# Two-layer hybrid decoder trunk: the last four chunks of the first layer's down product become two block pairs

## The chip, the cores and the metric

The program runs on one core of one Trainium2 chip. The metric is the device time of one execution in microseconds (us). A core has a matrix engine (PE, with its weight loads shown apart as PEld), VectorE (DVE), ScalarE (ACT), GpSimd (POOL) and SyncE (SP), which here issues nearly all DMAs. Each engine works through its own list of instructions in order and waits on semaphores for the others. PE multiplies a 128x128 weight tile by a moving tile of up to 512 columns and writes into PSUM, which has eight banks of 128x512 numbers here.

## The reference

Batch 1, 512 tokens, width 1024, two layers. Each layer ends in the MLP, of which the change touches the second product; the next layer begins with a norm and a projection of the same `x`:

```python
def hybrid_layer(x, g_mix, w_in, sinks, w_a, w_b, w_out, g_mlp, w_up, w_down):
    h = rmsnorm(x, g_mix)
    z = h @ w_in
    ...
    x = x + mixed @ w_out
    h2 = rmsnorm(x, g_mlp)
    x = x + jnp.square(jax.nn.relu(h2 @ w_up)) @ w_down     # w_up 1024x4096, w_down 4096x1024
    return x
```

## The kernel before

**Layout.** Activations lie transposed: `x` is 8 chunks of 128 rows (channels) by 512 columns (tokens), in SBUF. Every factor of a product is a pair of tiles, `hi` (the value rounded to the type that PE takes) and `lo` (the rest), and one product is three matmuls: hi by hi, hi by lo, lo by hi (`products`, L332 to L334). So one output chunk over 1024 channels is 24 matmuls of 512 columns.

**Weights.** They come in units of 128x1024. `unit_order` lists the units in the order in which they are used; `load_until` issues their DMAs into `raw` tiles (three buffers), and `split_until` makes `hi` on ACT (L286) and `lo` on DVE (L287), three units ahead of use.

**The MLP.** The 4096 hidden channels are done in four quarters. `mlp_sequence` alternates a pair of w_up chunks of quarter q+1 with two w_down chunks of quarter q. The hidden values of a quarter are called u in the code (`up[q]`): a raw tile `z` of two chunks, squared on ACT and split into `hi` and `lo`. Only the last quarter's w_down product stands alone. In layer 0 it is `group` for output chunks 0 to 3 (four units, four PSUM banks open at once, 96 matmuls) and then `chunk` for 4, 5, 6 and 7. The tail of each chunk is `put_down(c, True)`: add the bank to `x` (DVE, L1436), `scaled_input` (a split of gain times x into the next layer's input, one ACT and one DVE instruction), `squared_input` (a square on ACT, an add on DVE) and a DMA of `x[c]` to HBM (`spill`). Layer 1 has its own ending, `end`.

**Block pairs.** For w_b, w_out and most of w_up the kernel has another form, `narrow_pair` (and `wide_pair`): two output chunks at once as a 2x2 block product with seven block products in place of eight. Tokens and channels are halved, so a block product is four channel tiles by 256 tokens; with three matmuls each, a narrow pair is 84 matmuls of 256 columns where two chunks are 48 of 512. It takes the weights in four parts, of which three halves are sums that DVE makes (`add_part`, L252 to L260, four 128x512 instructions a pair), and it takes three combined forms of the moving side, made by `sum_input` from the raw tiles (four 128x512 adds on DVE, then two splits of 128x1024 on ACT and DVE), which is called twice for 1024 channels. It uses three PSUM banks, `a`, `b` and `e`: `a` is filled first, copied into `b` by ACT, and the rest is added up in these banks and in two SBUF tiles.

**PSUM and order.** `ps_mm` has five banks, `ps_aux` three. The order on each engine is not the order of the code: the program is built with a scheduler that places every instruction by a timeline of its own, so what stands where must be read from the built program. Waits are found from the buffers.

Of the kernel before, what the change touches and what calls it, by code (L numbers as in the profile page):

```python
# [18 lines left out]
P = 128  # L19
T = 512  # L20
D = 1024
KD = D // P
DEPTH = 2
# [7 lines left out]
D_FF = 4096  # L31
# [19 lines left out]
ASIDE = 48  # L51
FIRST_WIDE, LAST_WIDE = 6, 32
BETWEEN = (0, 2, 4, 5)
PARKED = (("w_b", 0), ("w_b", 2), ("w_out", 6), ("w_up", 4), ("w_up", 6))
H = T // 2
CROSSED = (0, 1, 4, 5, 2, 3, 6, 7)


def unit_order():

    def plain(name, *at):
        return [(name, i) for i in range(*at)]

    def pairs(src, *firsts):
        return [("pair", j, part, src) for j in firsts for part in range(4)]

    order = plain("w_in", 26) + plain("w_a", 4) + plain("w_in", 26, 46)
    order += pairs("w_b", 0, 2) + plain("w_b", 4, 8)
    order += plain("w_out", 2) + pairs("w_out", 2, 4, 6)
    for what, q, i in mlp_sequence():  # L70
        if what == "first":
            order += plain("w_up", 4)
        elif what == "pair":
            order += pairs("w_up", 8 * q + 2 * i)
        elif what == "down":
            order += plain("w_down", 8 * q + 2 * i, 8 * q + 2 * i + 2)
        else:
            order += plain("w_down", 8 * q, 8 * q + 8)
    return order


# [46 lines left out]
def decoder(ctx, tc, xT, x_first, w_in, w_a, w_b, w_out, w_up, w_down, tables, decay, band, triangles, g_last, out):  # L128
# [34 lines left out]
    spill, aside = (dram.tile([P, KD, T], F32, name=n) for n in ("spill", "aside"))  # L163


    order = [(layer, *u) for layer in range(DEPTH) for u in unit_order()]
    raws, parts, homes = {}, {}, []
    state = {"next": 0, "loaded": 0, "split": 0}

# [433 lines left out]
    def layer_body(layer):  # L603
# [722 lines left out]
        form = form_of(by_form)  # L1326

        up = [[] for _ in range(4)]
        up_slots = [[] for _ in range(4)]

        def put_up(ps):
# [80 lines left out]
        def pair(q, i, late):  # L1412

            c = 8 * q + 2 * i
            pool = ps_aux if i % 2 == 0 else ps_mm
            turn = iter(range(7))

            def step(ins):
                now = next(turn)
                while late and now == BETWEEN[4 - len(late)]:  # L1420
                    with tc.issue_after(ins), tc.issue_after(last_low[0]):
                        late.pop(0)()

# [28 lines left out]
        for what, q, i in mlp_sequence():  # L1452
            if what == "first":
                late = group("w_up", layer, xs, [put_up] * 4, first_hooks())
            elif what == "pair":
                pair(q, i, late)
                if (q, i) == (3, 3):
                    old_input()
                    for t, _ in homes_x:
                        slots.give(*t[1])  # L1460
            elif what == "down":
                if (layer, q, i) == (DEPTH - 1, 2, 2):
                    turning = turns(0)
# [12 lines left out]
    new_input()  # L1476
# [73 lines left out]
def _swapped(u):  # L1550
    return np.concatenate([u[:, UNIT // 2 :], u[:, : UNIT // 2]], 1)
# [34 lines left out]

def _half_grouped(w):
    r = np.arange
    return _units_group(w, r(T)) + _units_chunks(w, T + r(T))


def _stack(w, of):
# [75 lines left out]
```

## Time and profile before

| what | value |
|---|---|
| median of three runs | 1468.94 us (1468.91 to 1469.76) |
| profiled execution, first to last instruction | 1467.5 us |
| granted clock of PE over the span | 1.000 |
| DVE, ACT busy over the span | 79%, 56% |
| last quarter of w_down, layer 0, first matmul of `group` | 688.55 us |
| last chunk's add to `x` | 733.70 us |
| first matmul of the sum for layer 1's norm (ssq) | 744.60 us |

The page gives the profiled execution by its span of 1467.5 us; the runs' median lies 1.4 us above it. In rows of the trace the first number is the start in us from the span's start, the second the duration, then engine, line, operation, tiles by name, shape; in brackets the idle time of the engine ahead of the instruction and what ended it. A matmul's end is modelled, so the distance from one matmul's start to the next is its cost. In rows of windows each engine has busy us and instruction count, then the granted clock, the DMA share and GB/s.

### The profile page before, as it was taken

What the parts mean: (1) busy time and instruction counts of PE and PEld (TensorE: products, weight loads), DVE (VectorE), ACT (ScalarE), POOL (GpSimd) and SP (SyncE); (2) the same over time, 40 slices, a digit from 0 to 9 for tenths busy, and PEclk for the clock granted to TensorE, in tenths of its full rate; (3) what the DMA queues carried; (4) which work ended last, traced back from release to release, by engine and by line L of the source; (5) the groups of instructions that cost most, each with busy time, mean ns of one, the idle gap of its engine ahead of it and who ended that gap; (6) DMA issues with size and microseconds to landing.
All of it is one profiled execution on the core that took longest, in us unless ns stands there. A gap on an engine that the chain in (4) does not pass through costs nothing.

```text
span 1467.5 us, 20166 instructions
## 1 busy us (share of the span) xinstructions
PE 1461.0 (100%) x7434; PEld 1246.4 (85%) x7434; DVE 1161.6 (79%) x1912; ACT 814.6 (56%) x1306; POOL 3.7 (0%) x14
## 2 busy tenths in 40 slices
PE   9999999999999999999999999999999999999998
PEld 7888888888988888888888888888989888888887
DVE  7998778678988787776678977786899877877774
ACT  7657356654684445444456653666547754455544
POOL 0000000000000000000000000000000000000000
PEclk9999999999999999999999999999999999999999
DMA  6423843356443332333543258323654432333373
GB/s 227 134 87 101 280 166 98 104 171 210 130 120 125 101 115 88 107 108 115 165 121 102 86 168 285 107 95 107 191 197 123 144 101 87 125 105 101 108 200 108
DMA packets 73346, 198.65 MB, mean 135 GB/s; under 512 B 8712, under 2 KB 8864, under 8 KB 73248
## 3 DMA queue, kind: packets, MB, share of 16 engines
q1 hardware_dynamic: 72960, 196.84, 42.5%
q8 instruction: 58, 0.95, 0.3%
q10 hardware_dynamic: 288, 0.52, 0.1%
q14 instruction: 40, 0.33, 0.1%
HBM read 173.73 MB, written 20.98 MB: 133 GB/s over the span
## 4 chain that ended last, share of the span: by engine, by line
PE 99%; DVE 0%; issue 0%; POOLq 0%; ACT 0%; DVEq 0%; ACTq 0%
PE mm L334 24%; PE mm L332 23%; PE mm L333 23%; PE mm L1356 11%; PE mm L1357 6%; PE rv L332 2%; PE rv L334 2%; PE rv L333 2%; PE score L864 1%; PE r L332 1%; PE r L334 1%; PE r L333 1%; PE pT L819 0%; PE pv L846 0%; PE pv L845 0%; PE warm L311 0%
## 5 line engine op out<-in xcount | busy, mean ns | idle before, releaser
L333 PE MATMUL mm<-r,hi 128*128 128x512 f32 (+1 forms) x1568 | 572.5, 367 | 0.0
L332 PE MATMUL mm<-r,hi 128*128 128x512 f32 (+1 forms) x1568 | 569.9, 367 | 0.0
L334 PE MATMUL mm<-r,lo 128*128 128x512 f32 (+1 forms) x1568 | 563.9, 367 | 0.2
L286 ACT ACTIVATE hi<-raw 128x1024 fp32r<-128x1024 f32 (+1 forms) x334 | 333.9, 1002 | 377.8 <-PE mm L333 206.9
L287 DVE TENSOR_TENSOR lo<-raw,hi 128x512 fp32r<-128x512 f32 (+1 forms) x335 | 384.3, 1150 | 110.8 <-ACT hi L286 109.4
L334 PEld LDWEIGHTS mm<-r,lo 128*128 128x128 f32 x1568 | 293.6, 188 | 48.8 <-DVE lo L287 1.4
L332 PEld LDWEIGHTS mm<-r,hi 128*128 128x128 f32 x1568 | 294.1, 188 | 46.5 <-ACT r L342 0.2
L333 PEld LDWEIGHTS mm<-r,hi 128*128 128x128 f32 x1568 | 294.3, 188 | 46.0
L1356 PE MATMUL mm<-r,hi 128*128 128x512 f32 x728 | 252.0, 391 | 0.0
L1357 PE MATMUL mm<-r,lo 128*128 128x256 f32 x728 | 200.3, 277 | 0.0
L1356 PEld LDWEIGHTS mm<-r,hi 128*128 128x128 f32 x728 | 136.5, 188 | 28.7 <-ACT mm L1383 0.2
L1357 PEld LDWEIGHTS mm<-r,lo 128*128 128x128 f32 x728 | 136.7, 188 | 3.2 <-DVE lo L287 0.6
L1429 ACT ACTIVATE z<-z 128x512 f32<-128x512 f32 x56 | 32.5, 624 | 51.8 <-DVE z L1409 51.8
L1436 DVE TENSOR_TENSOR x<-x,mm 128x512 f32<-128x512 f32 x56 | 37.7, 686 | 28.1 <-PE mm L334 28.1
L334 PE MATMUL rv<-hi,r 128*128 128x512 f32 x128 | 49.8, 389 | 0.0
L333 PE MATMUL rv<-lo,r 128*128 128x512 f32 x128 | 49.8, 389 | 0.0
L332 PE MATMUL rv<-hi,r 128*128 128x512 f32 x128 | 49.8, 390 | 0.0
L339 ACT ACTIVATE r<-z 128x512 fp32r<-128x512 f32 x64 | 38.5, 619 | 16.3 <-DVE z L1090 16.1
L340 DVE TENSOR_TENSOR r<-z,r 128x512 fp32r<-128x512 f32 x64 | 42.9, 685 | 4.7 <-ACT r L339 4.3
L891 ACT ACTIVATE sm<-sm,st 128x256 f32<-128x256 f32 (+1 forms) x64 | 30.1, 472 | 19.0 <-DVE st L879 18.8
L1409 DVE SCALAR_TENSOR_TENSOR z<-z,rstd 128x512 f32<-128x512 f32 x52 | 35.6, 685 | 0.6
L340 DVE TENSOR_TENSOR r<-sums,r 128x1024 fp32r<-128x1024 f32 x24 | 28.9, 1216 | 0.0
(270 smaller groups left out, 1679.2 us busy)
## 6 DMA issues: line engine op xcount, KB each, us to landing
raw<-w_in_in SPq DMA_DIRECT2D x89, 512.0 KB, 3.6
raw<-w_down_in SPq DMA_DIRECT2D x64, 512.0 KB, 3.6
raw<-w_up_in SPq DMA_DIRECT2D x32, 512.0 KB, 3.9
raw<-w_up_in SPq DMA_DIRECT2D x60, 256.0 KB, 2.9
raw<-w_a_in SPq DMA_DIRECT2D x8, 512.0 KB, 6.5
ahead<-w_b_in SPq DMA_DIRECT2D x8, 512.0 KB, 5.4
park_w_b<-ahead SPq DMA_DIRECT2D x16, 256.0 KB, 5.9
ahead<-w_up_in SPq DMA_DIRECT2D x8, 512.0 KB, 5.7
```

Of the source, the lines that this page charges most:

```text
L286: nc.scalar.activation(hi[:, at], raw[:, at], AF.Copy)
L287: last_low[:] = [nc.vector.tensor_tensor(lo[:, at], raw[:, at], f32(hi[:, at]), ALU.subtract).ins]
L332: nc.tensor.matmul(ps, ah, bh, start=start and i == 0, stop=False, **more)
L333: nc.tensor.matmul(ps, ah, bl, start=False, stop=False, **more)
L334: nc.tensor.matmul(ps, al, bh, start=False, stop=stop and i == n - 1, **more)
L339: nc.scalar.activation(hi, src, AF.Copy)
L340: nc.vector.tensor_tensor(lo, src, f32(hi), ALU.subtract)
L1356: nc.tensor.matmul(both, hi[:, c], m, start=start and k == 0, stop=False, **more)
L1357: nc.tensor.matmul(ps[:, :H], lo[:, c], m[:, 0, :], start=False, stop=k == 3 and start, **more)
L1409: nc.vector.scalar_tensor_tensor(z[:, :, at], z[:, :, at], 0.0, factor, ALU.max, ALU.mult)
L1429: nc.scalar.activation(z[:, i, :], z[:, i, :], AF.Square)
L1436: nc.vector.tensor_tensor(x[:, c, :], x[:, c, :], ps, ALU.add)
```

## The change

In layer 0, last quarter, chunks 4 to 7 of the w_down product become two narrow pairs (4, 5) and (6, 7). The weights of these four units are stored with every second unit's halves swapped, and listed as pairs. The raw tiles of u of this quarter are kept: the first three go to HBM (into `aside`) as they are made and come back (`again`), the fourth stays in SBUF; from them `sum_input` makes the three combined forms into four groups of slots. The tail of a chunk (`finish_x`) is delayed and let in at two places within the next pair. Layer 1 is as it was.

```diff
+FIRST_LATE = 4
...
-            order += plain("w_down", 8 * q, 8 * q + 8)
+            order += plain("w_down", 8 * q, 8 * q + FIRST_LATE) + pairs("w_down", *range(8 * q + FIRST_LATE, 8 * q + 8, 2))
...
             up_slots[q].extend(own)
+            if q == 3 and layer < DEPTH - 1:
+                if c < D_FF // P - 2:
+                    nc.sync.dma_start(aside[:, c - 24 : c - 22, :], z)
+                else:
+                    last_up.append(z)
...
             else:
+                delayed.clear()
+                homes_u = [forms_home() for _ in range(4)]
+                by_form_u = [h[1] for h in homes_u]
+
+                def again(k):
+                    two = big("again")
+                    nc.sync.dma_start(two, aside[:, k : k + 2, :])
+                    return two
+
+                sum_input(by_form_u, [again(0), again(4)], 0)
+                sum_input(by_form_u, [again(2), last_up[0]], 2)
                 new_input()
                 all_of(group("w_down", layer, up[q], [put_down(c, True) for c in range(4)]))
-                for c in range(4, KD):
-                    chunk("w_down", layer, up[q], put_down(c, True))
+
+                def block_u(half, tokens):
+                    at = slice(tokens * H, tokens * H + H)
+                    return [tuple(m[:, at] for m in up[q][k]) for k in range(4 * half, 4 * half + 4)]
+
+                def finish_x(c):
+                    scaled_input(c, g_mix + 2)
+                    squared_input(c, g_mix + 2)
+                    nc.sync.dma_start(spill[:, c, :], x[:, c, :])
+
+                for c in range(FIRST_LATE, KD, 2):
+                    narrow_pair(ps_aux if c % 4 else ps_mm, delayed_step(), form_of(by_form_u), block_u, add_to_x(c))
+                    delayed.extend(partial(finish_x, c + i) for i in range(2))
+                all_of(delayed)
+                delayed.clear()
+                for t, _ in homes_u:
+                    slots.give(*t[1])
                 slots.give(*up_slots[q])
```

Three places in the built programs matter. Lines of the changed kernel are numbered 3 or 4 higher than before (L287 becomes L290, L1436 becomes L1445).

The first is DVE's list behind the last scaling of u with 256 tokens (L1409, L1413). `lo`, `raw` and `z` are weight rest, weight tile and u's raw tile; `sums` are u's combined forms. Before:

```order
862 L1409 SCALAR_TENSOR_TENSOR z<-z,rstd 128x2x256
863 L287 TENSOR_TENSOR lo<-raw,hi 128x1024
864 L1363 TENSOR_TENSOR z<-mm,side 128x256
865 L287 TENSOR_TENSOR lo<-raw,hi 128x1024
866 L1409 SCALAR_TENSOR_TENSOR z<-z,rstd 128x2x256
867 L287 TENSOR_TENSOR lo<-raw,hi 128x1024
868 L340 TENSOR_TENSOR r_80<-z,r_80 128x512 x2
869 L287 TENSOR_TENSOR lo<-raw,hi 128x1024
870 L1436 TENSOR_TENSOR x<-x,mm 128x512 x3
```

Now, from the same instruction on:

```order
862 L1413 SCALAR_TENSOR_TENSOR z<-z,rstd 128x2x256
863 L629 TENSOR_TENSOR sums<-again 128x512
864 L632 TENSOR_TENSOR sums<-again 128x512
865 L630 TENSOR_TENSOR sums<-again,sums 128x512
866 L633 TENSOR_TENSOR sums<-again,sums 128x512
867 L343 TENSOR_TENSOR r_84<-sums,r_84 128x4x256
868 L629 TENSOR_TENSOR sums<-again 128x512
869 L343 TENSOR_TENSOR r_89<-sums,r_89 128x4x256
870 L290 TENSOR_TENSOR lo<-raw,hi 128x1024
871 L1367 TENSOR_TENSOR z<-mm,side 128x256
872 L290 TENSOR_TENSOR lo<-raw,hi 128x1024
873 L1413 SCALAR_TENSOR_TENSOR z<-z,rstd 128x2x256
```

Seven instructions of the forms stand ahead of the weight split that was next before, and the third tile from HBM (row 868) is read ahead of it.

The second is further down the same list: from the first weight sum of the pair (4, 5) to the adds of the group's banks to `x`. Of these rows only a split, the two of u (r_80) and the adds stood there before.

```order
876 L632 TENSOR_TENSOR sums<-z,again 128x512
877 L258 TENSOR_TENSOR raw_6415<-raw 128x512
878 L343 TENSOR_TENSOR r_80<-z,r_80 128x512
879 L633 TENSOR_TENSOR sums<-z,sums 128x512
880 L343 TENSOR_TENSOR r_80<-z,r_80 128x512
881 L262 TENSOR_TENSOR raw_6539<-raw 128x512
882 L263 TENSOR_TENSOR raw_6539<-raw_6415 128x512
883 L290 TENSOR_TENSOR lo<-raw,hi 128x1024
884 L343 TENSOR_TENSOR r_82<-sums,r_82 128x4x256
885 L290 TENSOR_TENSOR lo<-raw_6415,hi 128x1024
886 L343 TENSOR_TENSOR r_86<-sums,r_86 128x4x256
887 L1445 TENSOR_TENSOR x<-x,mm 128x512 x3
```

Ahead of these rows stand 874 (L255, the first weight sum) and 875 (L630, a form), both of 128x512. The adds of the group's banks now stand behind 13 instructions that begin with row 874; before, they stood behind one split and the two of u.

The third is PE at the end of the group, where the first pair begins. Before, chunk 4 began in the fifth bank among the last matmuls of the group (r_80 is u's last tile, r_87 its first):

```order
3530 L332 MATMUL mm<-r_87,hi 128x512 [waits DVE_49,Activation_49]
3531 L333 MATMUL mm<-r_87,hi 128x512
3532 L332 MATMUL mm<-r_80,hi 128x512 [waits Activation_49]
3533 L332 MATMUL mm<-r_80,hi 128x512 x3
3534 L334 MATMUL mm<-r_87,lo 128x512 [waits DVE_49]
```

Now the pair's bank `a` begins there with two matmuls and goes on with the ten below, and bank `e` is begun right behind it (r_84 is a form of u):

```order
3551 L337 MATMUL mm<-r_87,lo 128x256 [waits DVE_49]
3552 L335 MATMUL mm<-r_87,hi 128x256
3553 L336 MATMUL mm<-r_87,hi 128x256
3554 L337 MATMUL mm<-r_87,lo 128x256
3555 L335 MATMUL mm<-r_83,hi 128x256
3556 L336 MATMUL mm<-r_83,hi 128x256
3557 L337 MATMUL mm<-r_83,lo 128x256
3558 L335 MATMUL mm<-r_83,hi 128x256
3559 L336 MATMUL mm<-r_83,hi 128x256
3560 L337 MATMUL mm<-r_83,lo 128x256
3561 L335 MATMUL mm<-r_84,hi 128x256 [waits DVE_49]
```

The wait of row 3561 is for a bank: `a`, `b` and `e` of this pair come from `ps_mm`, whose five banks hold the group's four, so `b` and `e` are banks of the group, and `e` is free when DVE has added the group's second bank to `x` (the second of row 887 above).

More of the change, by code (lines that the diff above doesn't have):

```diff
@@ L56, with unit_order @@
 CROSSED = (0, 1, 4, 5, 2, 3, 6, 7)
-def unit_order():
+def unit_order(last):
     def plain(name, *at):
@@ L76, in unit_order @@
             order += plain("w_down", 8 * q + 2 * i, 8 * q + 2 * i + 2)
+        elif last:
+            order += plain("w_down", 8 * q, 8 * q + 8)
         else:
-            order += plain("w_down", 8 * q, 8 * q + 8)
+            order += plain("w_down", 8 * q, 8 * q + FIRST_LATE) + pairs("w_down", *range(8 * q + FIRST_LATE, 8 * q + 8, 2))
     return order
@@ L163, in decoder @@
     spill, aside = (dram.tile([P, KD, T], F32, name=n) for n in ("spill", "aside"))
-    order = [(layer, *u) for layer in range(DEPTH) for u in unit_order()]
+    order = [(layer, *u) for layer in range(DEPTH) for u in unit_order(layer == DEPTH - 1)]
     raws, parts, homes = {}, {}, []
@@ L1328, in layer_body @@
         up = [[] for _ in range(4)]
+        last_up = []
         up_slots = [[] for _ in range(4)]
@@ L1588, in _half_grouped @@
     r = np.arange
-    return _units_group(w, r(T)) + _units_chunks(w, T + r(T))
+    paired = _units_chunks(w, r(FIRST_LATE * P, D))
+    return _units_group(w, r(T)) + [_swapped(u) if i % 2 else u for i, u in enumerate(paired)]
 def _stack(w, of):
```

## The prediction

> **What bounds the kernel now.** I read the page's shares and chain first, then windows over the stretch that changes, then the single rows there.
>
> ```profile
> PE 1461.0 (100%) x7434; PEld 1246.4 (85%) x7434; DVE 1161.6 (79%) x1912; ACT 814.6 (56%) x1306; POOL 3.7 (0%) x14
> PE 99%; DVE 0%; issue 0%; POOLq 0%; ACT 0%; DVEq 0%; ACTq 0%
> 690.94:738.50 47.56, 47.56 (x214) 39.42 (x213) 28.99 (x39) 21.49 (x31) 0.00 (x0) 1.00 0.49 159
> 370.00:412.00 42.00, 41.91 (x304) 39.36 (x303) 38.32 (x56) 30.60 (x48) 0.00 (x0) 1.00 0.38 111
> ```
>
> PE is the chain: 99% of it, and the third row has PE busy for all 47.56 us of the last quarter, at clock 1.00. So a matmul saved there is time saved, and a wait of PE there is time lost. DVE works 28.99 of the 47.56 us (61%). The fourth row is the w_out product, three narrow pairs with the same tails as the new ones: DVE at 38.32 of 42.00 us (91%), and PE still has next to no gap. That is the best case for the change, and the mark to compare DVE's new load with.
>
> **What PE saves.** Out go 4 x 24 = 96 matmuls of 512 columns, in come 2 x 84 = 168 of 256.
>
> ```profile
> 728.26 0.69 DVE L1436 TENSOR_TENSOR x<-x,mm 128x512 f32<-128x512 f32 x1 [2.03 <-PE mm L334]
> 733.70 0.69 DVE L1436 TENSOR_TENSOR x<-x,mm 128x512 f32<-128x512 f32 x1 [2.04 <-PE mm L334]
> 372.44 0.28 PE L332 MATMUL mm<-r,hi 128*128 128x256 f32 x1
> 379.51 0.28 PE L332 MATMUL mm<-r,hi 128*128 128x256 f32 x1
> L333 PEld LDWEIGHTS mm<-r,hi 128*128 128x128 f32 x1568 | 294.3, 188 | 46.0
> ```
>
> Two chunks end 733.70 - 728.26 = 5.44 us apart: 24 matmuls, 0.2267 each. In w_out 60 narrow matmuls lie between 372.44 and 379.51: 0.1178 each. So 168 x 0.1178 - 96 x 0.2267 = 19.79 - 21.76 = **-1.97 us**, the whole gain, 0.13% of the time. Weight loads take 188 ns a piece but overlap, as the spacing of 0.1178 shows. The Trainium skill ("TensorE: Matmul & The Clock Gate", section "The mechanism", the list of what overlaps) says that weight loads overlap running matmuls only when row groups differ; with its figure of 107 ns for 128 columns ("LDWEIGHTS (loading the stationary operand)") beside the matmuls, an estimate would be 168 x 0.107 - 96 x 0.107 = 7.7 us more, so 5.7 us slower in all. By that rule 0.1178 could not be; the trace disagrees, and the sum goes by the row.
>
> **What DVE gets.** These rows give its pace: the distance between starts, back to back.
>
> ```profile
> 716.20 1.22 DVE L287 TENSOR_TENSOR lo<-raw,hi 128x1024 fp32r<-128x1024 f32 x1
> 717.34 0.74 DVE L343 SCALAR_TENSOR_TENSOR r<-x,r 128x512 fp32r<-128x512 f32 x1
> 718.00 0.68 DVE L429 TENSOR_TENSOR acc<-acc,sq 128x512 f32<-128x512 f32 x1
> 718.60 0.68 DVE L1436 TENSOR_TENSOR x<-x,mm 128x512 f32<-128x512 f32 x1
> 668.01 0.41 DVE L1368 TENSOR_TENSOR bu<-bu,mm 128x256 f32<-128x256 f32 x1
> 668.34 0.41 DVE L1368 TENSOR_TENSOR eu<-eu,mm 128x256 f32<-128x256 f32 x1
> 690.94 0.68 DVE L1409 SCALAR_TENSOR_TENSOR z<-z,rstd 128x512 f32<-128x512 f32 x1
> 697.02 1.23 DVE L287 TENSOR_TENSOR lo<-raw,hi 128x1024 fp32r<-128x1024 f32 x1 [5.40 <-ACT hi L286]
> 706.30 0.39 PE L332 MATMUL mm<-r,hi 128*128 128x512 f32 x1
> ```
>
> 1.14 us for 1024 columns, 0.66 for a scaled split, 0.60 for 512, 0.33 for 256. Added are two `sum_input` (each 4 x 0.60 + 2 x 1.14 = 4.68), per pair four weight sums (2.40) and one and a half more units of splits (3 x 1.14 + 0.60 - 2 x 1.14 = 1.74), and small adds in place of two large ones (4 x 0.33 + 0.60 - 1.20 = 0.72): 9.36 + 2 x 4.86 = 19.1 us. Counted row by row in the new order, from behind the scaling at 690.94 to the last row that the second pair needs: 15 of 1024, 8 scaled splits, 32 of 512 and 8 of 256, 17.1 + 5.3 + 19.2 + 2.6 = 44.2 us. PE's own work to that point ends, without any wait, at 706.30 (u's last tile begins) + 24 x 0.2267 + 19.79 + 24 x 0.2267 (matmuls of the next layer that the order puts ahead of the pair's last twelve) = 737.0, so DVE has 737.0 - 691.5 = 45.4 us: 97% where w_out has 91%, if DVE never waits. It does wait, for two landings.
>
> ```profile
> 686.05 0.33 SPq L196 DMA_DIRECT2D raw<-w_down_in  x1
> 686.43 0.43 SPq L689 DMA_DIRECT2D rawtab<-tables_in  x1
> raw<-w_down_in SPq DMA_DIRECT2D x64, 512.0 KB, 3.6
> gate<-aside SPq DMA_DIRECT2D x8, 512.0 KB, 5.1
> ```
>
> **First stall, the bank.** The first two reads of `aside` follow the weight load of 686.05, in the place of `rawtab`, so at about 686.5 and 686.9. A like pair, the gates, lands after 5.1 us; behind a third transfer I take 692.5 for the second. DVE's row 864 then ends at 693.2, and its tile is what the third read needs (`big` goes round), so that read lands 3.6 to 5.1 us later, 697.3 in the middle. DVE's row 868 waits for it at the head of the list, and rows 868 to 870 end at 697.3 + 0.60 + 1.14 + 1.22 = 700.3. Row 870 frees the raw tile for the pair's second weight chunk: 3.6 us later, 703.9, row 874 may start. From there to the end of the second add of row 887 are nine rows of 512, four of 1024 and two adds: 5.4 + 4.6 + 1.2 + 0.1 = 11.3 us, so 715.2. PE wants that bank at 706.30 + 24 x 0.2267 + 12 x 0.1178 = 713.15. Wait: **2.0 us**. Lower bound 0: row 870 cannot end before 698.3, since its buffer kept it until 697.02 before too, and then 698.3 + 3.6 + 11.3 = 713.2 is just in time. Upper bound 3.5, with 5.1 us for both late landings; I take 2.2.
>
> **Second and third stall, ACT and DVE behind it.** From the end of the first add, D, the order gives ACT three scalings, four squares and three other things before the copy that frees `e`.
>
> ```profile
> 712.43 0.73 ACT L342 ACTIVATE r<-x 128x512 fp32r<-128x512 f32 x1 [5.10 <-DVE x L1436]
> 713.06 0.62 ACT L425 ACTIVATE acc<-x 128x512 f32<-128x512 f32 x1
> 713.59 0.71 ACT L342 ACTIVATE r<-x 128x512 fp32r<-128x512 f32 x1
> 696.89 0.36 ACT L1362 ACTIVATE side<-mm 128x256 f32<-128x256 f32 x1
> 697.16 1.05 ACT L286 ACTIVATE hi<-raw 128x1024 fp32r<-128x1024 f32 x1
> 379.63 0.28 PE L333 MATMUL mm<-r,hi 128*128 128x256 f32 x1
> 379.91 0.39 PE L334 MATMUL mm<-r,lo 128*128 128x256 f32 x1
> 380.13 0.28 PE L332 MATMUL mm<-r,hi 128*128 128x256 f32 x1
> ```
>
> 0.63 a scaling, 0.53 a square or half split, 0.27 a copy of 256. Four scalings, four squares, a half split and a copy are 5.4 us, and the copy that counts 0.4: D + 5.8. PE, let go at D + 0.7, has 36 narrow matmuls before it needs that copy: D + 4.9, so it waits **0.9**. DVE after D: three adds and a weight sum, 2.4, then a split, four scaled splits, a weight sum, two adds to acc, half a split, a small add and one more split: 1.14 + 2.64 + 0.6 + 1.2 + 0.6 + 0.33 + 1.22 = 7.7, so the weight rest of pair (6, 7) is ready at D + 10.2. PE needs it 26 narrow matmuls after D + 5.8, at D + 8.9: **1.3**. Behind that the next rests are due 38 and 22 narrow matmuls apart (4.5 and 2.6 us) and DVE has 3.6 and 2.1 us of rows for them: no more waits. Each wait also costs the next matmul its overlap: 379.63 to 379.91 to 380.13 is 0.28 and 0.22 where 0.12 is the pace, so 0.1 on top, **0.3** for three. Below nothing this cannot go: both sums lack any idle time and hang on D alone.
>
> **Behind the end.** ACT's new work (forms, 4 x 0.97; weights, 3 x 0.96) hides: 21.49 of 47.56 us now. So do three writes and three reads of 512 KB, but for the landings above; spills move with the tails and are read back only in layer 1's w_out; `rawtab` now loads among layer 1's first weights on SP's list, and is used only behind `ssq`.
>
> ```profile
> 744.60 0.39 PE L478 MATMUL ssq<-sh,ones 128*128 128x512 f32 x1
> 750.01 1.23 DVE L690 TENSOR_TENSOR tab<-rawtab,rstd 128x1024 f32<-128x1024 f32 x1
> 753.64 0.60 ACT L695 ACTIVATE rot<-mm 64x512 f32<-64x512 f32 x1 [2.52 <-PE mm L334]
> 756.00:780.00 24.00, 24.00 (x112) 19.90 (x111) 22.18 (x49) 18.99 (x37) 0.00 (x0) 1.00 0.49 143
> ```
>
> The new order puts `ssq` behind 80 matmuls of layer 1's first group instead of 49, 31 x 0.2267 = 7.0 us later. The tables were ready at 751.2, 2.4 ahead of the first bank; now they come about 4 after it. The next chunk has the fifth bank and 5.4 us, so no wait there. But DVE (22.18 of 24.00 us) starts some 4 us behind. I take **0.5 us** for a later wait, between 0 and 2 (most of the lag stays in DVE's gaps).
>
> **The sum.** -1.97 + 2.2 + 0.9 + 1.3 + 0.3 + 0.5 = +3.2 us. The profiled span of 1467.5 becomes 1470.7; what lies around it, 1.4 us up to the median of the runs, stays: 1468.94 + 3.2 = **1472.2 us**. With the first stall at its ends and layer 1 at 0 to 2: 1469.5 to 1475.0.
>
> **The rivals.**
> - *DVE keeps up* (w_out's rows speak for it, at 91% with gaps of a few tenths; 97% and the shared banks against it). If the landings are early and the tails do not hold PE: 1468.94 - 1.97 + 0.3 = 1467.3. Half way, first stall 0 and the two behind it in full: 1469.5. This side is not slower, and it decides at D: if the second add ends before 713.1 only 0.5 us remains, within the measurement.
> - *The trip through HBM is late.* Each us by which the third read lands after 697.3 moves row 874, D and all behind it by one. If both late landings take 2.5 us more than taken: 1477. For it: four transfers of 512 KB meet there; against it: DMA share is 0.49.
> - *Layer 1 pays.* If DVE's lag of 4 us is not absorbed by gaps before the background work must be done, PE waits for it all in place of 0.5: 1475.7. Against it: the 1.8 us of gaps in 24.
> - *Weight loads pace the narrow matmuls* at 188 ns: 168 x 0.188 - 21.76 = +9.8, 1478.7: what the rule named above would mean here. The w_out rows say no.
>
> **How the numbers follow.** What a measurement can tell from no change is about 0.2%, 2.9 us: 1466.0 to 1471.9. The forecast with its own range, 1469.5 to 1475.0, has 0.66, of which 0.40 lies above 1471.9; DVE keeps up has 0.16, late trip 0.09, layer 1 0.08, weight loads 0.01. Slower: 0.40 + 0.17 (the last three but a little) = 0.57; faster 0.03, since 1.97 us is not 2.9 and only a luckier order elsewhere could give it; same 0.40. Range 1468.5 to 1476.0.
>
> **What would show it.** Right: PE idle ahead of the first matmul of `mm<-r_84` at about 713, released by DVE's add to `x`, about 2 us; then waits for an ACT copy and for a `lo` of DVE, of 0.9 and 1.3; DVE without gaps from 704 to 725, and a gap before the read of the third `again`. Wrong: PE without gaps there and the span 2 us shorter; or a wait of several us in the attention of layer 1, after 760; or narrow matmuls further apart than 0.118.

## The result, and the profile after

| what | before | changed |
|---|---|---|
| median of 13 runs each | 1469.12 us (1468.51 to 1469.76) | 1472.28 us (1471.31 to 1472.51) |
| ratio | | 1.002, 95% interval 1.0013 to 1.0028 |
| profiled execution, first to last instruction | 1467.5 us | 1469.9 us |
| the profiled execution's time as a run | | 1471.65 us |

The change makes the kernel slower by 3.2 us, about 0.2%. The profiled execution of the changed kernel is 0.6 us below the median of its runs, and the two spans differ by 2.4 us only. Part of that is how they begin: the matmuls up to the first one of `group` are the same, and the changed kernel's profile reaches it at 688.06 us, the other at 688.55. Counted from that matmul to the end of the span, it takes 781.8 us in place of 779.0: +2.8.

The page's shares, and the shares of the chain that ended last:

```profile
PE 1459.4 (99%) x7506; PEld 1247.8 (85%) x7506; DVE 1180.2 (80%) x1942; ACT 823.7 (56%) x1320; POOL 3.7 (0%) x14
PE 95%; DVE 3%; DMA 1%; issue 1%; ACT 1%; POOLq 0%; SPq 0%; DVEq 0%; ACTq 0%
```

PE's busy time fell by 1.6 us (1461.0 before), yet the span grew, and the chain that was 99% PE now runs through DVE, DMA and ACT for a few per cent. So PE saves about what it should and then waits. The timeline of PE shows where (start, duration, line, tiles; in brackets the idle time ahead of the matmul and what ended it):

```profile
712.47 0.28 PE L336 MATMUL mm<-r,hi 128*128 128x256 f32 x1
712.59 0.28 PE L337 MATMUL mm<-r,lo 128*128 128x256 f32 x1
714.53 0.38 PE L335 MATMUL mm<-r,hi 128*128 128x256 f32 x1 [1.67 <-DVE x L1445]
714.76 0.28 PE L336 MATMUL mm<-r,hi 128*128 128x256 f32 x1
...
718.76 0.28 PE L337 MATMUL mm<-r,lo 128*128 128x256 f32 x1
719.70 0.39 PE L335 MATMUL mm<-uhi,hi 128*128 128x256 f32 x1 [0.66 <-ACT eu L668]
...
722.75 0.28 PE L336 MATMUL mm<-r,hi 128*128 128x256 f32 x1
723.99 0.39 PE L337 MATMUL mm<-r,lo 128*128 128x256 f32 x1 [0.96 <-DVE lo L290]
```

Matmuls of 256 columns start 0.12 us apart, as in the first two rows. The distance 712.59 to 714.53 is 1.94 (1.95 before the starts are rounded), so this wait costs 1.83 beyond the pace; the next two cost 0.82 and 1.12. The brackets name the releasers that the prediction named, in its order: the add to `x` that frees a bank, the copy into `eu`, the weight rest of pair (6, 7). The first matmul after each wait starts its successor 0.1 late (714.53 to 714.76). Together that is 3.77 + 0.3 = 4.1 us in the last quarter. A wait in layer 1's attention is the only other new one above 0.2 us (view of the waits of PE, 780 to 960 us: us in total, times, longest):

```profile
PE mm L335 <- DVE z L995: 0.3, 1, 0.3
```

By the distance of starts it costs 0.6 with its restart. 4.7 - 1.97 = +2.7 us, where the trace has +2.8 from the first matmul of `group` on.

Why DVE is late is in its own timeline:

```profile
692.15 0.69 DVE L632 TENSOR_TENSOR sums<-again 128x512 f32<-128x512 f32 x1 [0.41 <-DMA again<-aside]
696.71 0.69 DVE L629 TENSOR_TENSOR sums<-again 128x512 f32<-128x512 f32 x1 [0.91 <-DMA again<-aside]
703.23 0.69 DVE L255 TENSOR_TENSOR raw<-raw 128x512 f32<-128x512 f32 x1 [1.49 <-DMA raw<-w_down_in]
713.20 1.87 DVE L1445 TENSOR_TENSOR x<-x,mm 128x512 f32<-128x512 f32 x3
```

and in two windows of the same stretch (busy us of PE, PEld, DVE, ACT, POOL with counts; then clock, DMA share, GB/s):

```profile
690.94:704.00 13.06, 13.06 (x62) 10.84 (x61) 9.81 (x14) 6.49 (x9) 0.00 (x0) 1.00 0.52 176
704.00:730.00 26.00, 22.70 (x158) 20.80 (x157) 26.00 (x38) 16.09 (x25) 0.00 (x0) 1.00 0.40 134
```

DVE loses 2.8 us to three landings, and from 704 to 730 it is busy for 26.00 of 26.00 us: what it lost it cannot make up. The add that PE waits for is the second of the row at 713.20 and ends at 713.20 + 0.60 + 0.68 = 714.48. The late read and the late weight chunk are issued when DVE frees their tiles, right behind the row at 692.15 and the split that runs from 698.45 to 699.67:

```profile
692.87 0.33 SPq L1485 DMA_DIRECT2D again<-aside  x1
699.70 0.33 SPq L228 DMA_DIRECT2D raw<-w_down_in  x1
```

### The profile page after: what moved, and what is told of

Same layout as the page of the kernel before. It is cut to its first block, busy times and chain, and to the rows that moved or that the text cites. A ratio compares the mean times of both kernels' runs of the same rounds, so it can differ in the third digit from the quotient of the medians.

```text
span 1469.9 us, 20366 instructions
## 1 busy us (share of the span) xinstructions
PE 1459.4 (99%) x7506; PEld 1247.8 (85%) x7506; DVE 1180.2 (80%) x1942; ACT 823.7 (56%) x1320; POOL 3.7 (0%) x14
## 4 chain that ended last, share of the span: by engine, by line
PE 95%; DVE 3%; DMA 1%; issue 1%; ACT 1%; POOLq 0%; SPq 0%; DVEq 0%; ACTq 0%
PE mm L337 22%; PE mm L335 22%; PE mm L336 22%; PE mm L1360 11%; PE mm L1361 5%; PE rv L335 2%; PE rv L337 2%; PE rv L336 2%; DVE lo L290 1%; PE score L867 1%; DMA again<-aside 1%; PE r L335 1%; PE r L337 1%; PE r L336 1%; PE pT L822 0%
## 5 line engine op out<-in xcount | busy, mean ns | idle before, releaser
L289 ACT ACTIVATE hi<-raw 128x1024 fp32r<-128x1024 f32 (+1 forms) x338 | 337.3, 1000 | 371.2 <-PE mm L336 204.6
L290 DVE TENSOR_TENSOR lo<-raw,hi 128x1024 fp32r<-128x1024 f32 (+1 forms) x339 | 387.9, 1147 | 103.1 <-ACT hi L289 101.3
L337 PEld LDWEIGHTS mm<-r,lo 128*128 128x128 f32 x1592 | 298.1, 188 | 49.1 <-DVE lo L290 2.5
L335 PEld LDWEIGHTS mm<-r,hi 128*128 128x128 f32 x1592 | 298.2, 188 | 48.6 <-DVE x L1445 1.9
L336 PEld LDWEIGHTS mm<-r,hi 128*128 128x128 f32 x1592 | 298.8, 188 | 44.9
L1360 PEld LDWEIGHTS mm<-r,hi 128*128 128x128 f32 x728 | 136.5, 188 | 28.7 <-ACT mm L1387 0.2
L1361 PEld LDWEIGHTS mm<-r,lo 128*128 128x128 f32 x728 | 136.7, 188 | 3.4 <-DVE lo L290 0.8
L1445 DVE TENSOR_TENSOR x<-x,mm 128x512 f32<-128x512 f32 x52 | 34.8, 685 | 20.9 <-PE mm L337 20.9
L1413 DVE SCALAR_TENSOR_TENSOR z<-z,rstd 128x512 f32<-128x512 f32 x52 | 35.6, 685 | 0.6
L343 DVE TENSOR_TENSOR r<-sums,r 128x1024 fp32r<-128x1024 f32 x28 | 33.7, 1214 | 0.4 <-ACT r L342 0.4
```

The source lines that it names most:

```text
L289: nc.scalar.activation(hi[:, at], raw[:, at], AF.Copy)
L290: last_low[:] = [nc.vector.tensor_tensor(lo[:, at], raw[:, at], f32(hi[:, at]), ALU.subtract).ins]
L335: nc.tensor.matmul(ps, ah, bh, start=start and i == 0, stop=False, **more)
L336: nc.tensor.matmul(ps, ah, bl, start=False, stop=False, **more)
L337: nc.tensor.matmul(ps, al, bh, start=False, stop=stop and i == n - 1, **more)
L343: nc.vector.tensor_tensor(lo, src, f32(hi), ALU.subtract)
```

## The experiments

All are edits of the changed kernel. Each was timed beside the kernel before on the same chip; the kernel before had a median of 1469.21 us beside e1 to e4, 1468.89 beside e5 to e7, 1469.11 beside e8 to e10 and 1469.51 beside e11 and e12.

| run | median us (range) | ratio to before, 95% interval |
|---|---|---|
| e1 pools swapped | 1472.42 (1471.85 to 1473.48) | 1.0022 (1.0012 to 1.0031) |
| e2 early reads | 1472.31 (1471.88 to 1472.73) | 1.0021 (1.0012 to 1.0029) |
| e3 one pair | 1469.29 (1468.16 to 1469.97) | 1.0000 (0.9991 to 1.0009) |
| e4 late tails | 1471.73 (1470.93 to 1474.51) | 1.0019 (1.0010 to 1.0028) |
| e5 sums on GpSimd | 1477.22 (1476.22 to 1477.56) | 1.0056 (1.0043 to 1.0068) |
| e6 early reads, late tails | 1471.91 (1469.40 to 1472.52) | 1.0017 (1.0008 to 1.0026) |
| e7 e5 and e6 together | 1474.04 (1473.66 to 1474.33) | 1.0035 (1.0023 to 1.0048) |
| e8 sums ahead | 1472.97 (1470.46 to 1474.29) | 1.0025 (1.0016 to 1.0033) |
| e9 sums ahead, late tails | 1469.39 (1468.62 to 1471.13) | 1.0005 (0.9996 to 1.0014) |
| e10 as e9, ps_aux | 1469.22 (1467.98 to 1473.11) | 1.0002 (0.9994 to 1.0011) |
| e11 as e10, loads spread | 1468.90 (1468.55 to 1471.22) | 1.0000 (0.9991 to 1.0008) |
| e12 as e11, 160 us earlier | 1469.36 (1468.82 to 1471.19) | 1.0001 (0.9992 to 1.0010) |

The theory: DVE has too much to do in one stretch, PE meets that lateness wherever it first needs something of DVE's or of ACT's behind it, and the narrow pairs are worth their 1.97 us where DVE is in time. The rivals: the choice of the bank, the trip of u through HBM, ACT's list, or the narrow pairs themselves.

### e1: is it the bank?

```diff
-                    narrow_pair(ps_aux if c % 4 else ps_mm, delayed_step(), ...
+                    narrow_pair(ps_mm if c % 4 else ps_aux, delayed_step(), ...
```

> Pair (4, 5) takes its three banks from ps_aux, which are free, and pair (6, 7) from ps_mm; nothing else moves but two neighbouring rows on DVE. Theory (DVE is late, and the bank is only the place where that shows first): the wait of 1.83 us for DVE's add to x is gone, but PE then comes 1.8 us earlier to the bank that ACT's copy into eu frees, and that copy comes no earlier, so the wait there grows from 0.82 to about 2.7 us, and the third stays near 1.1 to 1.9. Time as the changed kernel's, 1472.3, within 0.4. Rival (the choice of the bank costs): the first wait and its restart are gone and the others stay as they are, 1.9 us less, 1470.4.

Of the instruction lists little else moved: two neighbouring rows of DVE changed places, and on ACT the pair's first copy out of a bank (L665) went ahead of a scaling and a square. The waits of PE from 690 to 780 us:

```profile
PE mm L335 <- ACT eu L668: 2.8, 1, 2.8
PE mm L337 <- DVE lo L290: 1.3, 1, 1.3
```

The wait for the bank is gone, and all of it is back at the next place: 2.8 at the copy where 0.7 was, and 1.3 at the weight rest. The time did not move. The bank is where the lateness showed, not what cost.

### e2: is it the trip through HBM?

```diff
+        def read_early():
+            for ks in ((0, 4), (2,)):
+                t, own = slots.four()
+                read_slots.extend(own)
+                for n, k in enumerate(ks):
+                    read_back[k] = f32(t[:, 2 * n : 2 * n + 2, :])
+                    nc.sync.dma_start(read_back[k], aside[:, k : k + 2, :])
...
+            if (layer, q, i) == (0, 3, 3):
+                read_early()
```

> The three tiles of u are read back some 20 us earlier, into r tiles that are free then, so that DVE waits for none of them. In the changed kernel DVE waited 0.41 and 0.91 us for these reads and 1.49 us for the weight chunk that was loaded behind them. Rival (the trip through HBM is late, and that is the price): all 2.8 us come back, the add to x ends before PE needs the bank, the first wait goes with its restart, 1470.4 or less. Theory (DVE's rows fill the stretch up to D, and the weight chunk is held back by its buffer anyway): the add to x ends only 0.2 to 0.9 us earlier, the first wait stays at 0.9 to 1.6 and the two behind it stay: 1471.4 to 1472.1.

DVE no longer waits for any read, and the add to `x` is no earlier. DVE's timeline has one large gap:

```profile
700.34 1.23 DVE L290 TENSOR_TENSOR lo<-raw,hi 128x1024 fp32r<-128x1024 f32 x1 [2.60 <-ACT hi L289]
```

and PE's waits from 690 to 780 us are these:

```profile
PE mm L335 <- DVE x L1457: 2.1, 1, 2.1
PE mm L337 <- DVE lo L290: 0.4, 1, 0.4
```

The 2.8 us that DVE had lost to landings it now loses to a weight split whose `hi` ACT could not write while PE still used its buffer (2.60 us) and to the next split (0.66). The scheduler also puts two rows of 512 columns more between the first weight sum and the adds. So the add that PE waits for ends at 715.0, 0.5 later than before this edit. The rival fell as far as this edit tests it: 1472.31, and not 1470.4 or less. Theory's 1471.4 to 1472.1 was a little low, since it took the add to be earlier. The wait for the copy into `eu` is missing, and the windows behind the first wait say why:

```profile
710.00:715.00 5.00, 3.01 (x14) 2.16 (x12) 5.00 (x8) 1.61 (x2) 0.00 (x0) 1.00 0.24 77
715.00:718.50 3.50, 3.43 (x16) 3.44 (x17) 3.50 (x6) 3.50 (x8) 0.00 (x0) 0.52 0.82 300
718.50:722.00 3.50, 3.50 (x31) 3.50 (x31) 3.50 (x7) 2.88 (x6) 0.00 (x0) 0.99 0.02 5
```

After 2.1 us without a matmul the granted clock is 0.52 for 3.5 us: 16 matmuls take 3.43 us where 16 x 0.1178 = 1.9 would do. So PE reached the copy only when it was done. Here the slow stretch took the place of a wait and did not add to the time: the weight rest that PE needs next let it go on at 724.5 (724.0 in the changed kernel), and DVE, which made it, had been busy for all 12.00 us of these windows. (The changed kernel's own profile has no such stretch behind its 1.67.)

### e3: do the pairs themselves cost?

```diff
-FIRST_LATE = 4
+FIRST_LATE = 6
...
+                for c in range(4, FIRST_LATE):
+                    chunk("w_down", layer, up[q], put_down(c, True))
...
-    return _units_group(w, r(T)) + [_swapped(u) if i % 2 else u ...
+    return _units_group(w, r(T)) + _units_chunks(w, r(T, FIRST_LATE * P)) + [_swapped(u) if i % 2 else u ...
```

> Chunks 4 and 5 stay chunks, and only 6 and 7 become a narrow pair, from ps_aux; the input forms of u are the same. Half of the matmuls' gain, 0.99 us; DVE loses 4.86 us of added rows, and gets 10.9 us more before a pair needs its forms, so theory expects no wait of PE in the last quarter: 1469.1 - 0.99 + 0 to 0.6 for layer 1 = 1468.1 to 1468.7. Rival (a narrow pair costs by itself, so that half of the change costs half): 1469.1 + 1.6 = 1470.7. Rival (the trip of u costs, and it is the same with one pair): 1470 or more.

The window of the whole quarter:

```profile
688.00:740.00 52.00, 52.00 (x274) 44.80 (x273) 44.62 (x64) 28.70 (x40) 0.96 (x1) 1.00 0.55 188
```

PE is busy for 52.00 of 52.00 us, with the same forms and the same trip of u. The profiled span is 1467.1, 0.4 below that of before, which is -0.99 + 0.6: the wait of layer 1 is there unchanged. The runs say no difference (1.0000), 3 us better than two pairs, but 1469.29 is 0.6 above the range that theory expected. Outside the span these executions have 2.0 us where the kernel before has 1.8; why was not looked for. Half of the change does not cost half: what costs is the second half of DVE's work and 10.9 us less time for it, which this run does not separate.

### e4 and e6: is it ACT's list?

```diff
-                all_of(group("w_down", layer, up[q], [put_down(c, True) for c in range(4)]))
+                all_of(group("w_down", layer, up[q], [put_down(c, c < 2) for c in range(4)]))
...
+                delayed.extend(partial(finish_x, c) for c in range(2, 4))
```

> Of the tails of chunks 0 to 3, those of 2 and 3 (scaling, square, spill) wait until the steps of pair (4, 5), as the tails of 4 and 5 wait for those of pair (6, 7). ACT then has two scalings and two squares fewer ahead of the copy into eu, 2.3 us. Rival (ACT's list is a price of its own): the second wait, 0.82, goes with its restart, and nothing takes its place: 1471.4. Theory (DVE is what is late): PE then comes 0.9 us earlier to the lo of pair (6, 7), which DVE brings at most 0.3 us earlier, so that the third wait grows from 1.12 to about 1.8: 1472.0, within 0.3. The first wait stays at 1.8 in both.

PE's waits from 690 to 780 us in e4, in an execution that was the longest of its eleven:

```profile
PE mm L335 <- DVE x L1445: 2.1, 1, 2.1
PE mm L337 <- DVE lo L290: 1.6, 1, 1.6
PE mm L336 <- DVE r L343: 0.8, 1, 0.8
```

The wait for ACT is gone, and the one for the weight rest grew from 1.0 to 1.6, as in e1 but one place further down. In this execution the second read of u landed late: DVE waited 2.15 us for it, 0.41 in the changed kernel. That put back all behind it, the first wait too, and it is why a form of u came late (the 0.8). So the rows are best counted from PE's restart at the bank:

```profile
717.69 0.38 PE L335 MATMUL mm<-r,hi 128*128 128x256 f32 x1 [2.14 <-DVE x L1445]
726.82 0.39 PE L337 MATMUL mm<-r,lo 128*128 128x256 f32 x1 [1.56 <-DVE lo L290]
```

From there to the restart at the weight rest it is 9.1 us, and 9.5 in the changed kernel (714.53 to 723.99). That is the 0.3 of the theory and not the 0.9 of the rival, in one execution each. The median of 1471.73 lies between the theory's 1472.0 and the rival's 1471.4 and does not separate them. e6 delays the tails of three chunks, 1 to 3 (`c < 1`, `range(1, 4)`), and has e2's early reads.

> The early reads of e2 together with late tails as in e4, but of chunks 1, 2 and 3. Theory: the rows before the add that frees the bank are still all on DVE, so the first wait stays at 1.8 to 2.2; behind it ACT has three scalings and three squares fewer, and DVE three scaled splits and two or three sums fewer, ahead of what PE needs, so both later waits are gone: 1472.3 - 0.9 - 1.2 = 1470.2, with the first at 2.2 1470.6. If the tails' rows only fall in front of the next thing that PE needs, as they did in e4, 1471.7 or more.

PE's waits in e6, same stretch:

```profile
PE mm L335 <- DVE x L1457: 2.1, 1, 2.1
```

Only the first wait is left, as expected, but the time is 1471.91. Again the wait drew the clock down: in this window 17 matmuls took 3.30 us in place of 2.0, at a clock of 0.50.

```profile
716.60:719.90 3.30, 3.30 (x17) 3.30 (x17) 3.26 (x5) 1.56 (x4) 0.00 (x0) 0.50 0.67 243
```

1471.9 - 1.3 is the 1470.6 that was expected. Here nothing behind the wait is late, so the slow stretch adds to the time: a wait can cost more than its length. The clock recorded for each run agrees: the six of 1471.9 and more have 0.998, as the profiled one, and the five of 1471.5 and less (the lowest are 1469.4 and 1470.3) have 0.999.

### e5 and e7: DVE's sums on another engine

```diff
     def add_part(i):
         part = order[i][3]
+        adder = nc.gpsimd if order[i][4] == "w_down" else nc.vector
...
-            nc.vector.tensor_tensor(raws[i][:, RIGHT], w2[:, RIGHT], w2[:, LEFT], ALU.add)
+            adder.tensor_tensor(raws[i][:, RIGHT], w2[:, RIGHT], w2[:, LEFT], ALU.add)
```

and so for the other three sums of a pair.

> The eight sums of the two pairs' weights go from DVE to GpSimd, which is idle; the reads and tails are as in the changed kernel. DVE has four rows of 0.60 us fewer before the add that frees the bank and four fewer behind it. Theory (DVE's rows set the add): it ends some 2.4 us earlier, 712.0 where PE wants the bank at 712.6, so that the wait for DVE's add to x is gone, and so is the one for the lo of pair (6, 7). ACT's list is not shorter: in the new order its copies for pair (4, 5) stand behind three scalings, three squares and a split, so there a wait of about 2.2 us takes their place: 1472.3 - 1.9 - 0.9 - 1.2 + 2.3 = 1470.6, from 1469.4 to 1471.2. What a GpSimd sum takes no row shows: its only arithmetic row is 0.82 us for 128 columns. If a sum of 512 took four times that, the splits behind a chain of three sums would come 8 us late: 1475 or more. Rival (DVE is not the bound, the trip or the banks are): the wait for the add to x stays near 1.8, 1472.3.

A miss of 6.6 us, by a price that no row had shown. Three rows of POOL's timeline in this kernel:

```profile
705.51 1.63 POOL L259 TENSOR_TENSOR raw<-raw 128x512 f32<-128x512 f32 x1
707.10 1.73 POOL L263 TENSOR_TENSOR raw<-raw 128x512 f32<-128x512 f32 x1
...
716.63 1.30 POOL L256 TENSOR_TENSOR raw<-raw 128x512 f32<-128x512 f32 x1 [6.11 <-DVE x L1446]
```

and of DVE's, where the second to the fourth ran beside such sums:

```profile
703.58 0.69 DVE L631 TENSOR_TENSOR sums<-z,sums 128x512 f32<-128x512 f32 x1 [1.22 <-ACT z L1434]
704.19 1.79 DVE L633 TENSOR_TENSOR sums<-z,again 128x512 f32<-128x512 f32 x1
705.90 1.78 DVE L344 TENSOR_TENSOR r<-z,r 128x512 fp32r<-128x512 f32 x1
707.61 1.77 DVE L634 TENSOR_TENSOR sums<-z,sums 128x512 f32<-128x512 f32 x1
...
715.54 2.47 DVE L1446 TENSOR_TENSOR x<-x,mm 128x512 f32<-128x512 f32 x4
```

The sum takes GpSimd 1.3 to 1.75 us (one of eight 2.9). Seven DVE instructions of 512 columns with both inputs in SBUF, each beside such a sum, take 1.75 to 1.79 us in place of 0.69 or 0.74: 1.1 us more each, where each of the eight sums had cost DVE 0.60. Beside the sum of 2.9 a split of 1024 columns kept its 1.21, so there it was the sum that took long. The adds to `x`, one input of which is in PSUM, keep their 0.60 (four in 2.47 us, the last of them beside the sum at 716.63). So DVE came later, not earlier, and PE's waits grew with it: 2.4 for the add to `x`, 2.5 for a copy, 1.7 for a rest. It fits the theory all the same: more lateness of DVE, more waits at the same places. e7 has these sums, e2's reads and e6's tails, and could not show what it was made for.

> Both pairs, with all three: sums on GpSimd, early reads, late tails of chunks 1 to 3. Theory (lateness of DVE, and of ACT behind it, is the whole price, and the narrow pairs are worth 1.97 us without it): waits of 0.2 to 0.8 us for the add to x and 0.2 for a lo remain, and 0.6 in layer 1: 1469.2 - 1.97 + 0.6 + 0.4 to 1.1 = 1468.2 to 1468.9, faster than the kernel before by 0.3 to 1.0 us. Rival (two narrow pairs cost by themselves, or GpSimd's sums hold up DVE): no better than e6, 1470 or more.

PE's waits in e7, 580 to 780 us:

```profile
PE mm L336 <- DVE x L1458: 3.2, 1, 3.2
PE mm L337 <- DVE r L344: 1.2, 1, 1.2
```

At 1474.04 it is 5 us above the expected range, which is the rival's case of sums that hold up DVE.

### e8 to e10: DVE's sums on DVE, at another time

```diff
+PARKED_LATE = (("w_down", 28), ("w_down", 30), )
...
+        def park_turns():
+            two = []
+
+            def load(at):
+                two[:] = raws_ahead(layer, *at)
+
+            def sums(at):
+                sums_ahead(*at, two)
+
+            return [partial(f, at) for at in PARKED_LATE for f in (load, sums)]
...
+                elif (layer, q, i) == (0, 1, 2):
+                    turning = park_turns()
```

The steps run inside `two_chunks`, 85 to 125 us ahead of the last quarter.

> The eight sums of the two pairs' weights stay on DVE but are made ahead, among the down products of the second quarter of u where DVE has some 5 of 20 us idle, and are parked in HBM as those of w_out and w_up are; each pair then loads 2 MB in place of 1. DVE's work in all is the same, and no other engine gets any. Theory (what is late is DVE in this one stretch): DVE has 2.4 us fewer before the add that frees the bank, which then ends at 712.0 to 712.3 at the latest, so the wait for the add is 0 to 0.2, and the lo of pair (6, 7) is in time too. The tails are as before, so ACT's copies still stand behind scalings and squares: one wait of 0.8 to 1.8 for ACT. 1472.3 - 4.1 + 0.9 to 2.0 = 1469.1 to 1470.2. Rival (the pairs cost by their traffic: more of it makes them slower): the two pairs' 2 MB more land late, 1473 or more. Rival (DVE's total is what counts, wherever its rows stand): 1472.3.

> The sums made ahead as in e8, and the tails of chunks 1 to 3 delayed as in e6, so that ACT has three scalings and three squares fewer ahead of its copies. Theory: what is left of the waits in the last quarter is 0 to 0.5 us; the narrow pairs' 1.97 us are there for the first time: 1469.1 - 1.97 + 0.6 (layer 1, as in the changed kernel) + 0 to 0.6 = 1467.7 to 1468.3, faster than the kernel before by 0.8 to 1.4 us. If it is 1469.0 or more, a price of the change is still not found.

> As e9, with both pairs from ps_aux, so that pair (6, 7) follows pair (4, 5) in the same three banks and the banks of ps_mm come free for layer 1. The later rows come in another order for it. Theory: the banks are no price once DVE is in time: within 0.4 of e9, 1467.5 to 1468.5. Rival (the second pair must wait until the first's last copies and adds have left the banks): a wait of 0.5 to 1.5 us at the second pair's first matmuls, 1468.7 to 1469.5.

PE's waits from 580 to 780 us, in e8:

```profile
PE mm L336 <- ACT mm L666: 1.8, 1, 1.8
PE mm L1361 <- ACT mm L1388: 0.2, 1, 0.2
```

in e9:

```profile
PE mm L336 <- ACT mm L666: 0.2, 1, 0.2
```

and in e10:

```profile
PE mm L1361 <- ACT mm L1388: 2.1, 1, 2.1
PE mm L336 <- ACT mm L666: 0.2, 1, 0.2
```

These traces are the main evidence. With the same sums on the same engine, only earlier (the scheduler places some other rows anew for it), the waits for DVE's add and for DVE's rest are gone in e8, and ACT's is left; with ACT's list shortened as well (e9) 0.2 us is left of all three. In e9 it is DVE that waits for PE ahead of the adds to `x`, and the quarter has both pairs and PE busy for 51.79 of 52.00 us:

```profile
710.78 2.05 DVE L1446 TENSOR_TENSOR x<-x,mm 128x512 f32<-128x512 f32 x3 [1.30 <-PE mm L338]
688.00:740.00 52.00, 51.79 (x311) 45.93 (x310) 45.26 (x64) 31.72 (x46) 0.96 (x1) 1.00 0.66 214
```

From the first matmul of `group` to the end of the span e9 takes 778.4 us, 0.6 less than the kernel before. That is -1.97 with 0.5 for the last wait and its restart, 0.3 for a short one and 0.6 in layer 1. But the runs give no gain: medians of 1469.39 and 1469.22 where 1467.7 to 1468.3 and 1467.5 to 1468.5 were expected. e9's profiled span of 1466.6 is the shortest of its eleven, and outside the span its executions have 2.1 us where the kernel before has 1.8, for a reason that was not looked for. e8, whose profiled execution of 1470.46 is its fastest, has 1472.97, about what its traffic rival said; e9 and e10 carry the same traffic and do not have it. e10's 1469.22 lies in the range of its rival, but the wait that this rival named, at the second pair's first matmuls, is not in the trace.

e10's profile caught a bad execution (1472.92, of a median of 1469.22). The wait of 2.1 in it is at 601 us, among the loads of the sums made ahead, and DVE's timeline shows what was late:

```profile
595.11 0.69 DVE L256 TENSOR_TENSOR raw<-raw 128x512 f32<-128x512 f32 x1 [5.44 <-DMA raw<-w_up_in]
```

Two chunks of 512 KB for the sums stand on SP's list right ahead of one of this wide pair's weight loads; DVE stood still for 5.44 us (0.25 in the kernel before), and behind PE's wait the granted clock was 0.52 from 604.0 to 607.4. So making the sums ahead costs a race of landings that some executions lose. In e10 these seem to be two of eleven: 1472.92 and 1473.11 are the only ones with a recorded clock below 0.999. Whether e8's slow median is the same loss was not shown; six of its eleven have 0.998, but its slowest, 1474.29, has not.

### e11 and e12: the loads spread out

In e11 the two loads of a pair are at two steps (`load(at, b)` for b = 0, 1, then `sums`), and the whole begins at (0, 2, 0); e12 is the same beginning at (0, 0, 0).

> As e10, but the weights for the sums are loaded one chunk at a time, at two steps of a down product, and 60 us later, in the third quarter of u. In e10's profile the two chunks of 512 KB stood on SP's list together, right ahead of a weight chunk that a wide pair then waited for: 2.26 us, and 3 us of half clock behind it, and nothing else of the change was left. Theory: with the burst halved that wait is gone or below 0.6, and no wait over 0.5 is left in the last quarter: 1469.1 - 1.97 + 0.4 to 1.0 = 1467.5 to 1468.2, faster than the kernel before by 0.9 to 1.6. Rival (the loads collide wherever they stand): a wait of 1 to 2.5 us for a weight chunk or for ACT's copy behind it, in that quarter, in most runs: 1469.0 or more.

> The same as e11 with the loads and sums in the first quarter of u, 160 us earlier, where the next thing that DVE and the queues have to do is the same kind of work. Theory: as e11, 1467.5 to 1468.4. If e11 is slow and this is not, it is the place of the loads; if both are slow, 1469.0 or more, making the sums ahead costs as much as the pairs bring.

In e11's trace PE has one wait of 0.2 us or more from 580 to 780, and not in the last quarter:

```profile
PE mm L1361 <- ACT mm L1388: 1.0, 1, 1.0
```

No wait above 0.2 us is left in the last quarter of either, and from the first matmul of `group` to the end of the span they take 777.8 and 777.7 us, 1.2 and 1.3 less than the kernel before. The loads take that back: from PE's 25th matmul, one of the first on weights, to the first of `group` it is 680.8 and 681.3 us where the kernel before has 679.7. A wait of 1.0 us among the loads is in e11, one of 0.7 in e12 (at 499.7, ahead of the view above), and some runs are at 1470 to 1471. 1468.90 and 1469.36 beside 1469.51 are no difference (1.0000 and 1.0001). So a wait of the kind that e11's rival named is there, with about 1 us, though its median lies between the two forecasts. No version was found that beats the kernel before by more than the measurement can tell.

## Why the prediction was right, step by step

**What PE saves, -1.97.** Right. e3 has half of it, 0.99, less the 0.6 in layer 1, and shows 0.4 in the span; e9 has all of it, less 1.4 of waits that its trace shows, and 0.6 is left from the first matmul of `group` on. Narrow matmuls were 0.12 apart with weight loads of 188 ns hidden under them; the rival by which weight loads set their pace fell, and with it the rule of the Trainium skill that the prediction weighed ("TensorE: Matmul & The Clock Gate", section "The mechanism"), for full-size tiles as here.

**First wait, 2.2 taken, 2.0 worked out.** 1.83. The third read landed at 696.7 (697.3 said), the weight chunk behind it at 703.2 (703.9), the second add ended at 714.5 (715.2): the whole chain of steps held, 0.7 early, of which 0.5 is that this execution reached the quarter earlier. (697.3 was not quite the middle: 3.6 to 5.1 us behind 693.2 is 696.8 to 698.3.) The lower bound of 0 did not hold where e2 tried it. The first weight sum then starts at 701.82, close to 698.3 + 3.6, but the wait of 0.66 and the two more rows of 512 columns stand between it and the add, which ends at 715.0 in place of 713.2.

**Second and third, 0.9 and 1.3.** 0.82 and 1.12. The rule "D + 5.8" for the copy, from the end of the first add at 713.9, gives 719.7, where PE went on; "D + 10.2" gives 724.1, and it was 723.99. That both hang on D alone was right: from there on neither ACT nor DVE has a gap before them. That they are one lateness, which moves on when a place is cleared, the prediction did not say; e1 and e4 show it.

**Restarts, 0.3.** 0.1 after each of three.

**Layer 1, 0.5.** The size came out (0.6), the reason did not. The prediction let DVE carry a lag of 4 us into the attention. e3 and e9 have DVE in time in the last quarter and the same wait for `z` (L995, in e9 L996) at the same place; in e10, e11 and e12, with another order of the rows of layer 1, it is not there. So it goes with the order that the scheduler made, and not with the lag. Which row of that order makes it was not looked for.

**The sum, +3.2.** The trace shows +2.8 from the first matmul of `group` on, the runs +3.2. That the median fits to a tenth is in part luck: the terms were 0.4 too large in the first wait, 0.1 and 0.2 in the other two, 0.1 too small in layer 1, and the runs lie 0.6 above the profiled execution. Some of that can be its early start. A drop of the clock in some of them, as in e6, would do it too: the clock on record is 0.998 in two of the six slowest (1472.40, 1472.51) and 1.000 in two of the four fastest (1471.31, 1471.79). But no trace of this kernel shows such a drop, so it is only argued.

**The rivals.** DVE did not keep up; e9 shows the quarter nearly as this rival had it, but its runs are at 1469.39 and not at 1467.3. The trip through HBM was not late (696.7 for the third read), and reading earlier brought nothing, with another wait in its place (e2); in e4's profile a read that came 1.7 us later did put back all behind it, as the rival said. Layer 1 paid 0.6, not the 4 us of DVE's lag.

## What to carry to other kernels

Where new work leaves an engine off the critical path almost no idle time (97% by count here, where 91% in w_out cost nothing), count its rows up to each deadline and add its landings; clearing the first place where its lateness shows only moves the wait to the next, so test by moving work out of the stretch, not by clearing the place. Before giving rows to an idle engine, look for a row that shows both engines working at once. And a change worth 2 us of 1469 is eaten by any wait or burst of loads that it needs, so look for the cheap half first: one pair here cost no wait in its quarter, though its 0.4 us in the trace is less than the runs can tell.

## What the runs showed that was not expected

**A short wait can halve the clock.** After 2.1 us without a matmul (e2, e6) the granted clock was 0.50 to 0.52 for 3.3 to 3.5 us; so it was in e10 behind 2.1, and in e7 behind 3.2 (0.57 from 717.8 to 721.2). In the profiled executions of e1, after 2.8, e4, after 2.1, and e5, after 2.4 and 2.5, it stayed at 1.00. The Trainium skill ("TensorE: Matmul & The Clock Gate", section "What's actually happening") has a free-running window of about 3.4 us whose idleness throttles PE; the length of the slow stretch agrees, and that it depends on where the wait falls would fit a free-running window. But 2.1 us, which is less than one such window, was enough here, and the page asks for a whole idle one.

**GpSimd slows DVE by more than it helps.** While GpSimd added 128x512 tiles, seven DVE instructions with two SBUF inputs took about 1.78 us in place of 0.69, some 7.7 us in all for eight sums of 0.60 taken off DVE; those with one input in PSUM took 0.60 as before. The Trainium skill ("GPSIMD Engine Reference", section "8. Key points") says that the two contend when DVE has two SBUF inputs; the trace agrees, and gives the price.
